# Splitting the shared rotary keys of a head pair as one bank, fifth score matmul over 64 rows, and shorter rsqrt chains in a single-core MLA kernel

## The chip, the cores and the metric

The kernel runs on one core of a Trainium2 chip. The metric is device time in microseconds of one execution. The core has a matrix engine (PE, with its weight loads listed apart as PEld), a vector engine (DVE), an activation engine (ACT), a general engine (POOL, also called GpSimd) and a sync engine (SP) whose queue issues nearly all DMAs. Each engine works through its own instructions in order; semaphores tie the engines together.

## The reference

Two layers over 512 tokens of width 2048: a pooling mixer, then multi-head latent attention with 16 heads. Only the attention matters here. Each head has 128 plain and 64 rotary channels; the rotary key is one for all heads, and the norm of a head's key runs over all 192 channels, so each head scales the same rotary key by its own factor.

```python
def shared_kv(x, kv_norm_g, kv_w_a, kv_latent_g, kv_w_b, k_norm_g, cos, sin):
    ...
    k_rope = jnp.broadcast_to(k_rope[:, :, None, :], (B, S, N_HEADS, QK_ROPE))
    k = qk_norm_rope(jnp.concatenate([k_nope, k_rope], axis=-1), k_norm_g, cos, sin)
    return k, v

def qk_norm_rope(t, g, cos, sin):
    t = rmsnorm(t, g)        # t * rsqrt(mean(t * t) + 1e-6) * g, over 192 channels
    return jnp.concatenate([t[..., :QK_NOPE], apply_rope(t[..., QK_NOPE:], cos, sin)], axis=-1)

def chunk_causal_attention(q, k, v):
    for i in range(S // QBLOCK):                 # QBLOCK 128
        s = jnp.einsum('bqhd,bkhd->bhqk', q[:, q0:k_end], k[:, :k_end]) * QK_HEAD ** -0.5
        ...
        p = jax.nn.softmax(s, axis=-1)
        outs.append(jnp.einsum('bhqk,bkhd->bqhd', p, v[:, :k_end]))
```

## The kernel before

All products are of float32 data that are split into a high and a low part (`hi` by a cast on ACT, `lo` = source - `hi` by a subtraction on DVE); a product is the sum of three matmuls, hi x hi, hi x lo and lo x hi. `split` (L154) does this for a whole tile.

The attention stage works on pairs of heads, `hg` = 0 to 7. The main loop (from about L1074) goes through 64 score units: pair, head `h` of the pair, block `i` of 128 queries. For each it emits the scores (`score_unit`), the exponential (`exp_unit`, ACT), the scaling by the reciprocal of the sum (`scale_unit`, DVE), the transposes of the scaled tile (`pt_unit`) and, for every second unit, the product with the values (`pv_unit`). Between these parts stand pieces of projections for the next pair (`kv_part`, `q_part`; in the last pair, pieces of the output projection), so that PE has work while the softmax runs. Preparations of the next pair are put at fixed units by the table `side`: `kstats_unit` behind unit 2, `krot_unit` behind unit 3, `tr_unit` 2 (the rotary keys) behind unit 5, `qstats_unit` and `tr_unit` 3 behind unit 6, `tr_unit` 5 (the rotary queries) in unit 7. The order of PE is that of the code, pinned by hand (`PINNED`). The order on ACT, DVE, POOL and SP is set by the tile scheduler, which places each instruction by its own model of when its inputs are there.

What the change touches:

- `kstats_unit` and `qstats_unit`, once a pair each: the factor 1/sqrt of 8 means per partition (4 token blocks x 2 heads), with `rsqrt` (L161): a first value by a shift of the float's bits, and three Newton steps of three instructions each (L166 to L168), on tiles of 128x8. With the scalings around it this makes 16 DVE instructions for k (four of them at L705, one for each token block) and 13 for q.
- `krot_unit` (L720, POOL) multiplies the shared rotary key by the factors of both heads, side by side in one tile.
- `tr_unit` with u = 2: four transposes (L754) put the rotary keys of both heads into one PSUM bank, head 0 in rows 0 to 63, head 1 in rows 64 to 127. Then, per head, two ACT casts of 64x512 (L763 and L764) write the high part twice, into rows 0 to 63 and 64 to 127 of a tile `kh`; DVE (L765) writes the low part into rows 0 to 63 of `kl`, and POOL (L762) zeros rows 64 to 127 of `kl`.
- `tr_unit` with u = 5: the rotary queries; per head one tile with the high part in rows 0 to 63 (L781) and the low part in rows 64 to 127 (L782).
- `score_unit` (L810): five matmuls into one bank. The first three are those of the plain channels. The fourth multiplies the tile of q (high over low) by `kh` (high over high), which gives two of the three rotary products at once; the fifth multiplies the same tile by `kl` (low over zeros).

`tr()` hands out two PSUM banks in turn to all transposes (of keys, queries and scaled tiles alike): a transpose waits until the bank's reader two uses before is through. `bt()` hands out 32 buffers of 128x512 in turn.

Numbers of lines are those of the kernel before; where a line of the changed kernel is meant, the text says so.

Of the kernel before, what the change touches and what calls it, by code (L numbers as in the profile page):

```python
# [7 lines left out]
F32 = mybir.dt.float32  # L8
F32R = mybir.dt.float32r
I32 = mybir.dt.int32  # L10
AF = mybir.ActivationFunctionType
ALU = mybir.AluOpType
AX = mybir.AxisListType

P = 128
S = 512
# [6 lines left out]
EPS = 1e-6  # L23
# [24 lines left out]
def trunk_kernel(  # L48
# [17 lines left out]
    V, A, G, T = nc.vector, nc.scalar, nc.gpsimd, nc.tensor  # L66

    const = ctx.enter_context(tc.tile_pool(name="const", bufs=1))
    rpool = ctx.enter_context(tc.tile_pool(name="rpool", bufs=2))
# [3 lines left out]
    def xt(shape=(P, S), dt=F32):  # L73
        return xpool.tile(list(shape), dt, tag="x", name="xt")
# [4 lines left out]
    def at(dt=F32R, shape=(P, S)):  # L79
        return apool.tile(list(shape), dt, tag="a", name="at")  # L80

    def bt(shape=(P, S), dt=F32R):
        return bpool.tile(list(shape), dt, tag="b", name="bt")
# [16 lines left out]
    def f(ap):  # L100
        return ap.bitcast(F32)
# [51 lines left out]
    def split(src, hi, lo):  # L153
        return A.copy(hi, src), V.tensor_tensor(lo, src, f(hi), ALU.subtract)  # L154
# [6 lines left out]
    def rsqrt(v, y, a, n):  # L161

        V.tensor_scalar(y.bitcast(I32), v.bitcast(I32), -0.5, float(0x5F3759DF), ALU.mult, ALU.add)
        V.tensor_scalar(v, v, -0.5, None, ALU.mult)
        for _ in range(3):
            V.tensor_tensor(a, y, y, ALU.mult)  # L166
            V.tensor_tensor(a, a, v, ALU.mult)
            V.scalar_tensor_tensor(y, a, 1.5, y, ALU.add, ALU.mult)  # L168
# [98 lines left out]
    with ExitStack() as c1:  # L267
# [106 lines left out]
        with ExitStack() as c2:  # L374
            hp = c2.enter_context(tc.tile_pool(name="hp", bufs=2, **tile_))
            for j in range(NJ):
# [5 lines left out]
                hi = w7.tile([P, 4, 2, P], F32R, tag="hi", name="hi")  # L382
                lo = w7.tile([P, 4, 2, P], F32R, tag="lo", name="lo")
# [10 lines left out]
                a, b = xh[j], xl[j]  # L394
# [11 lines left out]
        for o in range(0, 4, 2):  # L406
            e = epool.tile([P, 7, H], F32, tag="e", name="e")
            for i in range(2):
                v = e[:, 2 * i:2 * i + 2, :]
# [16 lines left out]
        for n, pair in enumerate((*range(18, 32), *range(16))):  # L426
# [7 lines left out]
            if n == 9:  # L434
                V.tensor_tensor(sq[0], sq[0], sq[1], ALU.add)
                p = ps7[0].tile([P, 2, H], F32, tag="k3", name="k3").rearrange("p h t -> p (h t)")
# [79 lines left out]
    for k in range(KD):  # L516
        hi, lo = at(), at()
        gsplit(xr[k], C_GKV + k, hi, lo)
        xkv.append((hi, lo))
        hi, lo = bt(), bt()  # L520
# [67 lines left out]
    kr = krb[:, 0:256].rearrange("p (t d) -> p t d", t=4)  # L588
# [6 lines left out]
    kr2 = const.tile([P, 4], F32, name="kr2")  # L595
# [34 lines left out]

    gqk = const.tile([P, 1], F32, name="gqk")
    V.tensor_tensor(gqk, cs[:, C_GKN:C_GKN + 1], cs[:, C_GQN:C_GQN + 1], ALU.mult)
    SC = 192.0 ** -0.5
    st, gated = {}, {}
    nhg = NH // 2

# [57 lines left out]
    def q_squares(hg, t):  # L694
        d = st[hg]
        for h in range(2):
            junk = spool.tile([P, 192], mybir.dt.bfloat16, tag="junk", name="junk", bufs=2)
            A.activation(junk, d["qraw"][t][:, h, :], AF.Square, accum_out=d["ssq"][:, 2 * t + h:2 * t + h + 1])

    def kstats_unit(hg):  # L700

        d = st[hg]
        v, a, y = small(8, "sv", 2), small(8, "sa", 2), small(8, "sy", 2)
        for t in range(4):
            V.tensor_scalar(v[:, 2 * t:2 * t + 2], d["ssk"][:, 2 * t:2 * t + 2], kr2[:, t:t + 1], None, ALU.add)  # L705
        V.tensor_scalar(v, v, 1.0 / 192, EPS, ALU.mult, ALU.add)
        rsqrt(v, y, a, 8)
        d["yk"] = y
        for a in range(2):
            kk = d["kraw"][a].rearrange("p b (h c) -> p (b h) c", h=2)  # L710
            V.tensor_tensor(kk, kk, y[:, 4 * a:4 * a + 4].unsqueeze(2).broadcast_to([P, 4, P]), ALU.mult)
# [11 lines left out]
    def qstats_unit(hg):  # L723

        d = st[hg]
        v, a, y = small(8, "qv", 2), small(8, "qa", 2), small(8, "qy", 2)
        V.tensor_scalar(v, d["ssq"], 1.0 / 192, EPS, ALU.mult, ALU.add)
        rsqrt(v, y, a, 8)
        V.tensor_scalar(y, y, SC, None, ALU.mult)
        d["rq"] = y  # L730

    def qrot_unit(hg, t):
# [13 lines left out]
    def tr_unit(hg, u):  # L746

        d = st[hg]
        if u == 2:

            d["kr"] = []
            p = tr()
            for t in range(4):
                T.transpose(p[:, t * P:(t + 1) * P], d["krs"][:, t * P:(t + 1) * P], ident)  # L754
            for h in range(2):
                src = p[h * 64:h * 64 + 64, :]
                if hg:
                    kh = bt()
                else:
                    kh = xt(dt=F32R) if h else rpool.tile([P, S], F32R, tag="r", name="kr0")  # L760
                kl = bt()
                G.memset(f(kl[64:128, :]), 0.0)  # L762
                A.copy(kh[0:64, :], src)  # L763
                A.copy(kh[64:128, :], src)  # L764
                V.tensor_tensor(kl[0:64, :], src, f(kh[0:64, :]), ALU.subtract)  # L765
                d["kr"].append((kh, kl))
            return
        p = tr()
        for t in range(4):
            if u < 2:  # L770
                src = d["kraw"][t // 2][:, t % 2, u * P:(u + 1) * P]
            elif u < 5:
                src = d["qraw"][t][:, u - 3, 0:128]
            else:
                src = d["qrot"][:, t * P:(t + 1) * P]
            T.transpose(p[:, t * P:(t + 1) * P], src, ident)  # L776
        if u == 5:
            q0, q1 = bt(), bt()
            for h, q in enumerate((q0, q1)):
                src = p[h * 64:h * 64 + 64, :]  # L780
                A.copy(q[0:64, :], src)  # L781
                V.tensor_tensor(q[64:128, :], src, f(q[0:64, :]), ALU.subtract)  # L782
            d["qr"] = (q0, q1)
            return
        ft = at if hg == 0 and u in (0, 3) else bt
        hi, lo = ft(), ft()
        if u in (3, 4):
            A.activation(hi, p, AF.Copy, scale=gqk)
            V.scalar_tensor_tensor(lo, p, gqk, f(hi), ALU.mult, ALU.subtract)
        else:  # L790
            split(p, hi, lo)
        d[("T", u)] = (hi, lo)

    def score_unit(hg, h, i):
        d = st[hg]
        n = (i + 1) * P
        if i == 2:

            gt = d[("G", h)] = bt(dt=F32)
            nc.sync.dma_start(gt, gates[2 * hg + h])  # L800
        s = sc()
        kh, kl = d[("T", h)]
        krh, krl = d["kr"][h]
        qh, ql_ = d[("T", 3 + h)]
        qr = d["qr"][h]
        qs = slice(i * P, (i + 1) * P)
        ops = [(qh[:, qs], kh[:, 0:n]), (qh[:, qs], kl[:, 0:n]), (ql_[:, qs], kh[:, 0:n]),
               (qr[:, qs], krh[:, 0:n]), (qr[:, qs], krl[:, 0:n])]
        for j, (l, r) in enumerate(ops):
            T.matmul(s[:, 0:n], l, r, start=(j == 0), stop=(j == 4))  # L810
        V.memset(s[0:64, n - 64:n], -1e30)
        nm = small(1, "nm", 4)
        V.tensor_reduce(nm, s[:, 0:n], AX.X, ALU.max)
        rq = d["rq"][:, 2 * i + h:2 * i + h + 1]
        V.scalar_tensor_tensor(nm, nm, -1.0, rq, ALU.mult, ALU.mult)
        d[("P", h, i)] = s, nm, rq
# [207 lines left out]
    for m, (key, w) in enumerate(keys):  # L1024
        n = last[keys[m - 4][0]] if m >= 4 else -1
# [48 lines left out]
    for m in range(len(seq) + 2):  # L1074
        now = seq[m] if m < len(seq) else None
        if now:
            hg, h, i = now
# [105 lines left out]
```

## Time and profile before

| what | us |
|---|---|
| runs | 1920.48, 1920.28, 1922.47 (median 1920.48) |
| the profiled execution | 1920.45 |
| its span, from first to last instruction | 1918.7 |
| attention stage, pairs 1 to 7 | about 1480 to 1765 of the span |
| one steady pair | 35.2 |

The profile is of one execution. Instructions are listed with the line that made them, the tile written and the tiles read, partitions x columns, a start and a duration. PE's instructions are pipelined: a matmul's listed duration overlaps the next, so the distance between two starts is what counts, and a distance longer than usual is a stall. Here are three stretches of the score loop, in windows (length; busy time and number of PE, PEld, DVE, ACT and POOL; clock; DMA share; GB/s):

```profile
1541.70:1577.00 35.30, 35.16 (x218) 31.69 (x218) 31.05 (x108) 27.43 (x91) 9.71 (x20) 1.00 0.25 79
1647.40:1682.60 35.20, 35.05 (x217) 31.67 (x216) 30.98 (x106) 27.35 (x90) 9.71 (x20) 1.00 0.27 83
1730.00:1765.00 35.00, 34.62 (x196) 29.98 (x195) 26.77 (x76) 19.23 (x49) 0.00 (x0) 1.00 0.43 124
```

The steady pairs are alike to a tenth of a microsecond. The last row is the last pair's second half, when no further pair is prepared; its POOL is empty.

### The profile page before, as it was taken

To read this page: it belongs to the slowest core of one execution; us is meant where nothing else is said; L and a number is where in the kernel's file an instruction comes from. 1 tells how busy PE (TensorE), PEld (TensorE's weight loads), DVE (VectorE), ACT (ScalarE), POOL (GpSimd) and SP (SyncE) were. 2 spreads that over 40 slices of the span, in tenths; PEclk is the share of its full clock that TensorE was granted. 3 is DMA by queue.
4 is the path that set the end of the run, shared out by engine and by line. 5 is a ranking of instruction groups with operands and counts; after the bars stand their busy time and mean duration, and the time that the engine had idled before them with its cause. 6 is when DMAs were issued, how large, how long until landed. Compare 5 with 4: busy or idle time off the path is not lost.

```text
span 1918.7 us, 30196 instructions
## 1 busy us (share of the span) xinstructions
PE 1902.5 (99%) x11084; PEld 1688.6 (88%) x11084; DVE 1299.6 (68%) x2282; ACT 829.2 (43%) x1555; POOL 286.9 (15%) x436
## 2 busy tenths in 40 slices
PE   8999999999999999999999999999999999999999
PEld 7999999999999988888888888888888888988887
DVE  8677796897766786586695576574335888887332
ACT  8444433333333442332432354233236787775221
POOL 0433343333232100000000000000001332320000
PEclk9999999999999999999999999999999999999999
DMA  6555444444454556334334344334443232244642
GB/s 191 158 162 159 150 132 133 123 129 138 145 151 131 167 172 199 115 119 152 118 124 137 105 150 132 93 99 121 116 120 95 82 96 77 74 128 143 200 117 87
DMA packets 177077, 251.24 MB, mean 131 GB/s; under 512 B 15776, under 2 KB 96800, under 8 KB 176928
## 3 DMA queue, kind: packets, MB, share of 16 engines
q1 hardware_dynamic: 176640, 249.10, 42.3%
q8 instruction: 87, 1.43, 0.3%
q14 instruction: 62, 0.51, 0.1%
q10 hardware_dynamic: 288, 0.20, 0.0%
HBM read 216.21 MB, written 33.03 MB: 130 GB/s over the span
## 4 chain that ended last, share of the span: by engine, by line
PE 93%; DVE 3%; DMA 2%; ACT 1%; issue 1%; POOL 0%; SPq 0%; DVEq 0%; POOLq 0%; ACTq 0%
PE mm L149 16%; PE mm L151 16%; PE mm L150 16%; PE k L346 10%; PE k L344 9%; PE k L342 9%; PE k L339 3%; PE sc L810 2%; PE mm L662 1%; PE mm L664 1%; PE mm L663 1%; PE mm L685 1%; PE mm L686 1%; PE mm L687 1%; PE tr L838 1%; PE tr L776 1%
## 5 line engine op out<-in xcount | busy, mean ns | idle before, releaser
L131 ACT CAST whi<-raw 128x512 fp32r<-128x512 f32 (+2 forms) x424 | 256.2, 607 | 539.4 <-PE mm L150 439.9
L132 DVE TENSOR_TENSOR wlo<-raw,whi 128x512 fp32r<-128x512 f32 (+2 forms) x424 | 283.8, 670 | 242.7 <-ACT whi L131 239.7
L346 PE MATMUL k<-xc,lo 128*128 128x256 f32 x1680 | 417.4, 283 | 0.8 <-DVE lo L320 0.8
L344 PE MATMUL k<-xc,hi 128*128 128x256 f32 x1440 | 397.5, 283 | 0.0
L342 PE MATMUL k<-xc,hi 128*128 128x256 f32 x1440 | 396.8, 282 | 0.0
L151 PE MATMUL mm<-bt,wlo 128*128 128x512 f32 x944 | 368.0, 390 | 0.0
L149 PE MATMUL mm<-bt,whi 128*128 128x512 f32 x944 | 367.7, 390 | 0.0
L150 PE MATMUL mm<-bt,whi 128*128 128x512 f32 x944 | 367.0, 389 | 0.0
L320 DVE TENSOR_TENSOR lo<-raw,hi 128x1792 fp32r<-128x1792 f32 x120 | 249.3, 2078 | 131.7 <-ACT hi L319 131.5
L319 ACT CAST hi<-raw 128x1792 fp32r<-128x1792 f32 x120 | 203.2, 1693 | 285.7 <-PE k L346 172.5
L346 PEld LDWEIGHTS k<-xc,lo 128*128 128x128 f32 x1680 | 302.7, 190 | 8.3 <-DVE lo L320 2.0
L342 PEld LDWEIGHTS k<-xc,hi 128*128 128x128 f32 x1440 | 273.3, 190 | 5.0
L344 PEld LDWEIGHTS k<-xc,hi 128*128 128x128 f32 x1440 | 273.7, 190 | 0.0
L151 PEld LDWEIGHTS mm<-bt,wlo 128*128 128x128 f32 x944 | 177.1, 188 | 37.3 <-issue 0.5
L149 PEld LDWEIGHTS mm<-bt,whi 128*128 128x128 f32 x944 | 177.3, 188 | 36.9 <-ACT whi L131 0.2
L150 PEld LDWEIGHTS mm<-bt,whi 128*128 128x128 f32 x944 | 177.2, 188 | 36.7
L150 PE MATMUL mm<-at,whi 128*128 128x512 f32 x432 | 168.6, 390 | 0.3 <-DVE at L154 0.3
L149 PE MATMUL mm<-at,whi 128*128 128x512 f32 x432 | 168.8, 391 | 0.0
L151 PE MATMUL mm<-at,wlo 128*128 128x512 f32 x432 | 168.2, 389 | 0.0
L315 POOL TENSOR_TENSOR raw<-raw 128x256 f32<-128x256 f32 x120 | 97.5, 812 | 428.3 <-DVE raw L313 410.1
L316 POOL TENSOR_TENSOR raw<-raw 128x256 f32<-128x256 f32 x120 | 110.0, 917 | 9.2
L150 PEld LDWEIGHTS mm<-at,whi 128*128 128x128 f32 x432 | 81.1, 188 | 17.3 <-DVE at L154 0.6
(1137 smaller groups left out, 2714.2 us busy)
## 6 DMA issues: line engine op xcount, KB each, us to landing
raw<-awin SPq DMA_DIRECT2D x240, 256.0 KB, 3.4
raw<-awo SPq DMA_DIRECT2D x128, 256.0 KB, 2.7
raw<-bwin SPq DMA_DIRECT2D x80, 256.0 KB, 2.9
raw<-awg SPq DMA_DIRECT2D x64, 256.0 KB, 2.7
scr<-e SPq DMA_DIRECT2D x56, 256.0 KB, 2.7
raw<-bwo SPq DMA_DIRECT2D x56, 256.0 KB, 2.9
raw<-wkvb SPq DMA_DIRECT2D x32, 256.0 KB, 3.1
raw<-wqb SPq DMA_DIRECT2D x32, 192.0 KB, 2.4
```

Source lines behind the costliest of these rows:

```text
L131: wsplits[:] = (A.copy(hi[:, :n], raw[:, :n]).ins, V.tensor_tensor(lo[:, :n], raw[:, :n], f(hi[:, :n]), ALU.subtract).ins)
L132: V.tensor_tensor(lo[:, :n], raw[:, :n], f(hi[:, :n]), ALU.subtract).ins)
L149: T.matmul(dst, wh, xh, start=first, stop=False)
L150: T.matmul(dst, wh, xl, start=False, stop=False)
L151: T.matmul(dst, wl, xh, start=False, stop=last)
L315: G.tensor_tensor(c[:, :, 6, :], c[:, :, 4, :], c[:, :, 2, :], ALU.add)
L316: G.tensor_tensor(c[:, :, 7, :], c[:, :, 6, :], c[:, :, 3, :], ALU.add)
L319: A.copy(hi, c[:, :, 1:8, :])
L320: V.tensor_tensor(lo, c[:, :, 1:8, :], f(hi), ALU.subtract)
L342: T.matmul(dst, hi[:, j % 2, wi, :], xh[j][:, xi, :], start=first, stop=False, skip_group_check=True)
L344: T.matmul(dst, hi[:, j % 2, wi, :], xl[j][:, xi, :], start=False, stop=False, skip_group_check=True)
L346: T.matmul(dst, lo[:, j % 2, wi, :], xh[j][:, xi, :], start=False, stop=last, skip_group_check=True)
```

## The change

It has three parts. **The split of the rotary keys** (`tr_unit`, u = 2): one cast and one subtraction take the whole bank of 128x512, with head 0 in the upper rows and head 1 in the lower. Three POOL copies of 64x512 then build what the fourth matmul needs: `k1` gets head 1's high part in both halves, and the lower half of `k0` is overwritten with head 0's; that last copy comes after DVE has read `k0`. `kl` holds the low parts of both heads; nothing is zeroed. A pair takes three `bt` buffers here, not four. **The fifth score matmul** reads 64 rows only: rows 0 to 63 for head 0, 64 to 127 for head 1. For that the queries of head 1 have their high part in rows 64 to 127 and the low part above it. **The rsqrt chains**: the factors -0.5, 1/192 and the eps are folded into one instruction per chain (with a constant tile `kr2b`, made once), and in place of three Newton steps come one step of a higher order, in four instructions, and one Newton step, in three. With the folding and the first value that makes 9 instructions for k and 9 for q.

```diff
@@ -630,7 +630,6 @@
 
     gqk = const.tile([P, 1], F32, name="gqk")
     V.tensor_tensor(gqk, cs[:, C_GKN:C_GKN + 1], cs[:, C_GQN:C_GQN + 1], ALU.mult)
-    SC = 192.0 ** -0.5
     st, gated = {}, {}
     nhg = NH // 2
 
@@ -697,14 +696,30 @@
             junk = spool.tile([P, 192], mybir.dt.bfloat16, tag="junk", name="junk", bufs=2)
             A.activation(junk, d["qraw"][t][:, h, :], AF.Square, accum_out=d["ssq"][:, 2 * t + h:2 * t + h + 1])
 
+    C3 = 3.375 ** 2
+    kr2b = const.tile([P, 4, 2], F32, name="kr2b")
+    V.tensor_scalar(kr2b, kr2.unsqueeze(2).broadcast_to([P, 4, 2]), -0.5 / (192 * C3), -0.5 * EPS / C3,
+                    ALU.mult, ALU.add)
+
+    def rsqrt_small(v, y, a):
+
+        V.tensor_scalar(y.bitcast(I32), v.bitcast(I32), -0.5, float(0x5F3759DF - 2 ** 30 - 2 ** 22),
+                        ALU.mult, ALU.add)
+        V.tensor_tensor(a, y, y, ALU.mult)
+        V.tensor_tensor(a, a, v, ALU.mult)
+        V.scalar_tensor_tensor(a, a, 5.0 / 3.0, a, ALU.add, ALU.mult)
+        V.scalar_tensor_tensor(y, a, 1.25, y, ALU.add, ALU.mult)
+        V.tensor_tensor(a, y, y, ALU.mult)
+        V.tensor_tensor(a, a, v, ALU.mult)
+        V.scalar_tensor_tensor(y, a, 2.0 / 3.0, y, ALU.add, ALU.mult)
+
     def kstats_unit(hg):
 
         d = st[hg]
         v, a, y = small(8, "sv", 2), small(8, "sa", 2), small(8, "sy", 2)
-        for t in range(4):
-            V.tensor_scalar(v[:, 2 * t:2 * t + 2], d["ssk"][:, 2 * t:2 * t + 2], kr2[:, t:t + 1], None, ALU.add)
-        V.tensor_scalar(v, v, 1.0 / 192, EPS, ALU.mult, ALU.add)
-        rsqrt(v, y, a, 8)
+        V.scalar_tensor_tensor(v, d["ssk"], -0.5 / (192 * C3), kr2b.rearrange("p t h -> p (t h)"),
+                               ALU.mult, ALU.add)
+        rsqrt_small(v, y, a)
         d["yk"] = y
         for a in range(2):
             kk = d["kraw"][a].rearrange("p b (h c) -> p (b h) c", h=2)
@@ -724,9 +739,8 @@
 
         d = st[hg]
         v, a, y = small(8, "qv", 2), small(8, "qa", 2), small(8, "qy", 2)
-        V.tensor_scalar(v, d["ssq"], 1.0 / 192, EPS, ALU.mult, ALU.add)
-        rsqrt(v, y, a, 8)
-        V.tensor_scalar(y, y, SC, None, ALU.mult)
+        V.tensor_scalar(v, d["ssq"], -0.5 / C3, -0.5 * 192 * EPS / C3, ALU.mult, ALU.add)
+        rsqrt_small(v, y, a)
         d["rq"] = y
 
     def qrot_unit(hg, t):
@@ -748,22 +762,19 @@
         d = st[hg]
         if u == 2:
 
-            d["kr"] = []
             p = tr()
             for t in range(4):
                 T.transpose(p[:, t * P:(t + 1) * P], d["krs"][:, t * P:(t + 1) * P], ident)
-            for h in range(2):
-                src = p[h * 64:h * 64 + 64, :]
-                if hg:
-                    kh = bt()
-                else:
-                    kh = xt(dt=F32R) if h else rpool.tile([P, S], F32R, tag="r", name="kr0")
-                kl = bt()
-                G.memset(f(kl[64:128, :]), 0.0)
-                A.copy(kh[0:64, :], src)
-                A.copy(kh[64:128, :], src)
-                V.tensor_tensor(kl[0:64, :], src, f(kh[0:64, :]), ALU.subtract)
-                d["kr"].append((kh, kl))
+            if hg:
+                k0, k1 = bt(), bt()
+            else:
+                k0, k1 = rpool.tile([P, S], F32R, tag="r", name="kr0"), xt(dt=F32R)
+            kl = bt()
+            split(p, k0, kl)
+            for half in (slice(0, 64), slice(64, 128)):
+                G.tensor_copy(k1[half, :], k0[64:128, :])
+            G.tensor_copy(k0[64:128, :], k0[0:64, :])
+            d["kr"] = (k0, kl[0:64, :]), (k1, kl[64:128, :])
             return
         p = tr()
         for t in range(4):
@@ -778,9 +789,10 @@
             q0, q1 = bt(), bt()
             for h, q in enumerate((q0, q1)):
                 src = p[h * 64:h * 64 + 64, :]
-                A.copy(q[0:64, :], src)
-                V.tensor_tensor(q[64:128, :], src, f(q[0:64, :]), ALU.subtract)
-            d["qr"] = (q0, q1)
+                hi, lo = q[h * 64:h * 64 + 64, :], q[64 - h * 64:128 - h * 64, :]
+                A.copy(hi, src)
+                V.tensor_tensor(lo, src, f(hi), ALU.subtract)
+            d["qr"] = (q0, q0[0:64, :]), (q1, q1[64:128, :])
             return
         ft = at if hg == 0 and u in (0, 3) else bt
         hi, lo = ft(), ft()
@@ -802,10 +814,10 @@
         kh, kl = d[("T", h)]
         krh, krl = d["kr"][h]
         qh, ql_ = d[("T", 3 + h)]
-        qr = d["qr"][h]
+        qr, qrh = d["qr"][h]
         qs = slice(i * P, (i + 1) * P)
         ops = [(qh[:, qs], kh[:, 0:n]), (qh[:, qs], kl[:, 0:n]), (ql_[:, qs], kh[:, 0:n]),
-               (qr[:, qs], krh[:, 0:n]), (qr[:, qs], krl[:, 0:n])]
+               (qr[:, qs], krh[:, 0:n]), (qrh[:, qs], krl[:, 0:n])]
         for j, (l, r) in enumerate(ops):
             T.matmul(s[:, 0:n], l, r, start=(j == 0), stop=(j == 4))
         V.memset(s[0:64, n - 64:n], -1e30)
```

PE's instructions stand in the same sequence as before. The order of the other engines moves. First ACT at a boundary between two steady pairs, where the rotary keys of the next pair are split: `bt<-tr 64x512` are the casts of the keys, `sc` the scores, `xt<-tr` the tiles of the transposed softmax. Before:

```order
L850 CAST xt<-tr 128x128
L763 CAST bt<-tr 64x512
L764 CAST bt<-tr 64x512
L823 ACTIVATE tt__15937,sm<-sc,nm,qy 128x256
L763 CAST bt<-tr 64x512
L764 CAST bt<-tr 64x512
L154 CAST at<-mm 128x256
L823 ACTIVATE tt__15993,sm<-sc,nm,qy 128x384
```

The same place in the changed kernel:

```order
L862 CAST xt<-tr 128x128
L154 CAST bt<-tr 128x512
L835 ACTIVATE tt__15887,sm<-sc,nm,qy 128x256
L154 CAST at<-mm 128x256
L835 ACTIVATE tt__15939,sm<-sc,nm,qy 128x384
```

One cast stands ahead of the exp of 256 columns where two stood, and none between it and the next exp. In the pair at 1505 us the one cast stands behind the exp of 256 columns, where the first of the four stood.

Second DVE at the same place. `qv`, `qy` and `qa` are the tiles of the q chain, `nm` the maximum of a score tile, `sm` the sum of an exp. Before:

```order
L727 TENSOR_SCALAR qv<-ssq 128x8
L852 TENSOR_TENSOR xt<-tr,xt 128x128
L163 TENSOR_SCALAR qy<-qv 128x8
L164 TENSOR_SCALAR qv<-qv 128x8
L166 TENSOR_TENSOR qa<-qy 128x8
L765 TENSOR_TENSOR bt<-tr,bt 64x512
L167 TENSOR_TENSOR qa<-qa,qv 128x8
L811 MEMSET sc 64x64
L829 RECIPROCAL sm<-sm 128x1
L168 SCALAR_TENSOR_TENSOR qy<-qa,qy 128x8
L813 TENSOR_REDUCE nm<-sc 128x1
L830 TENSOR_SCALAR tt__15937<-tt__15937,sm 128x256
```

In the changed kernel:

```order
L742 TENSOR_SCALAR qv<-ssq 128x8
L864 TENSOR_TENSOR xt<-tr,xt 128x128
L706 TENSOR_SCALAR qy<-qv 128x8
L154 TENSOR_TENSOR bt<-tr,bt 128x512
L708 TENSOR_TENSOR qa<-qy 128x8
L841 RECIPROCAL sm<-sm 128x1
L823 MEMSET sc 64x64
L709 TENSOR_TENSOR qa<-qa,qv 128x8
L842 TENSOR_SCALAR tt__15887<-tt__15887,sm 128x256
L825 TENSOR_REDUCE nm<-sc 128x1
L710 SCALAR_TENSOR_TENSOR qa<-qa 128x8
```

The scaling of the exp tile (L830, now L842) has moved ahead of the search for the next maximum (L813, now L825). In the pair at 1505 us it stands ahead of the subtraction of the keys in both kernels.

Third DVE in the last pair, around 1722 us, from the subtraction for an output weight on (`wlo`). Before:

```order
L132 TENSOR_TENSOR wlo<-raw,whi 128x256
L166 TENSOR_TENSOR qa<-qy 128x8
L811 MEMSET sc 64x64
L765 TENSOR_TENSOR bt<-tr,bt 64x512
L813 TENSOR_REDUCE nm<-sc 128x1
L167 TENSOR_TENSOR qa<-qa,qv 128x8
L815 SCALAR_TENSOR_TENSOR nm<-nm,qy 128x1
L168 SCALAR_TENSOR_TENSOR qy<-qa,qy 128x8
L166 TENSOR_TENSOR qa<-qy 128x8
L167 TENSOR_TENSOR qa<-qa,qv 128x8
L765 TENSOR_TENSOR bt<-tr,bt 64x512
```

In the changed kernel:

```order
L132 TENSOR_TENSOR wlo<-raw,whi 128x256
L154 TENSOR_TENSOR bt<-tr,bt 128x512
L712 TENSOR_TENSOR qa<-qy 128x8
L823 MEMSET sc 64x64
L713 TENSOR_TENSOR qa<-qa,qv 128x8
L825 TENSOR_REDUCE nm<-sc 128x1
L714 SCALAR_TENSOR_TENSOR qy<-qa,qy 128x8
```

The reading of the keys' bank ends with the one subtraction, at the place of the first L765; the second, seven rows later, is gone.

On POOL the memsets, which waited for nothing but a free buffer, are gone; the three copies stand behind the pair's last rotary query (L744, now L758) and wait for ACT's cast, the third for DVE's subtraction too. `krot_unit`'s two products come ahead of the last instruction of a rotary query, not behind it. On SP two things change, both late: a load of a gate comes ahead of a load of the output weights, and a store of a gated tile behind a load of another.

## The prediction

> **What bounds the kernel now.** I read the engines' busy line first, then the table by windows, then every gap between starts on PE from 1480 us on (where the pairs of heads follow each other), and last the timeline around those gaps.
>
> ```profile
> span 1918.7 us, 30196 instructions
> PE 1902.5 (99%) x11084; PEld 1688.6 (88%) x11084; DVE 1299.6 (68%) x2282; ACT 829.2 (43%) x1555; POOL 286.9 (15%) x436
> ```
>
> PE is busy for 99% of the span, so work that is taken from DVE or ACT is worth nothing by itself. Only a place where PE stands still for one of them can pay. The windows of the attention stage (columns: length, then the busy time and count of PE, PEld, DVE, ACT and POOL, the clock, DMA share, GB/s) say how much there is:
>
> ```profile
> 1577.00:1612.20 35.20, 35.06 (x218) 31.66 (x216) 30.98 (x107) 27.36 (x91) 9.70 (x20) 1.00 0.29 87
> 1682.60:1730.00 47.40, 44.77 (x266) 39.26 (x265) 41.94 (x144) 36.67 (x112) 9.44 (x20) 1.00 0.40 126
> ```
>
> A steady pair lasts 35.20 us, of which PE is busy for 35.06; the granted clock is 1.00, so no time can come back from there. The stretch into the last pair has 2.63 us without PE. Each of its stalls has to be looked at alone. The largest two have the same cause, the split of the rotary keys (ACT L763 and L764, DVE L765, each once per head):
>
> ```profile
> 1506.50 0.57 ACT L763 CAST bt<-tr 64x512 fp32r<-64x512 f32 x1
> ...
> 1509.01 0.39 PE L664 MATMUL mm<-wlo,at 128*128 128x512 f32 x1
> 1509.67 0.69 DVE L765 TENSOR_TENSOR bt<-tr,bt 64x512 fp32r<-64x512 f32 x1
> 1510.51 0.63 PE L776 MATMUL tr<-cs,qt 128*128 128x128 f32 x4 [1.11 <-DVE qy L168]
> ...
> 1721.88 0.68 DVE L765 TENSOR_TENSOR bt<-tr,bt 64x512 fp32r<-64x512 f32 x1
> ...
> 1722.71 0.38 PE L838 MATMUL tr<-cs,tt__18213 128*128 128x128 f32 x2
> 1723.81 0.69 DVE L765 TENSOR_TENSOR bt<-tr,bt 64x512 fp32r<-64x512 f32 x1
> 1724.65 0.63 PE L776 MATMUL tr<-cs,qt 128*128 128x128 f32 x4 [1.56 <-DVE qy L168]
> ```
>
> L776 transposes into one of the two `tr` banks, and the bank it gets is the one that the second L765 still reads. That L765 ends at 1510.36 and 1724.50, and PE goes on 0.15 us behind it. (The name behind the arrow, L168, is the small instruction that happened to end nearest; it writes nothing that L776 reads.) Two matmuls of 512 columns start 0.23 us apart when nothing holds them, so the first stall is 1.50 - 0.23 = 1.27 us. Two transposes of 128 columns take 0.17 us of PE (L838 at 1580.03, the next matmul at 1580.20, in the fence below), so the second is 1.94 - 0.17 = 1.77 us. **Together 3.04 us.**
>
> In the five pairs between, the same split costs less and by another way:
>
> ```profile
> 1576.95 0.58 ACT L763 CAST bt<-tr 64x512 fp32r<-64x512 f32 x1 [0.81 <-PE tr L754]
> 1577.54 0.58 ACT L764 CAST bt<-tr 64x512 fp32r<-64x512 f32 x1
> 1578.14 0.56 ACT L823 ACTIVATE tt__15937<-sc,nm,qy 128x256 f32<-128x256 f32 x1
> 1578.15 0.68 DVE L765 TENSOR_TENSOR bt<-tr,bt 64x512 fp32r<-64x512 f32 x1 [0.55 <-ACT bt L764]
> 1579.49 0.40 PE L664 MATMUL mm<-wlo,at 128*128 128x512 f32 x1
> 1579.54 0.34 DVE L830 TENSOR_SCALAR tt__15937<-tt__15937,sm 128x256 f32<-128x256 f32 x1
> 1580.03 0.41 PE L838 MATMUL tr<-cs,tt__15937 128*128 128x128 f32 x2
> ...
> 1580.20 0.48 PE L662 MATMUL mm<-whi,at 128*128 128x512 f32 x1
> ```
>
> The exp of the tile stands on ACT behind two casts, its scaling (L830) on DVE behind L765, and the transposes of that tile (L838) start at 1580.03 instead of 1579.49 + 0.23 = 1579.72: 0.31 us. The other four pairs read alike (L664 to L838 is 0.53 or 0.54 us), so **1.5 us in all**. What the kernel can gain from the split is at most 3.04 + 1.54 = 4.6 us.
>
> **The change part by part.** *The split.* Per pair, four casts of 64x512 become one of 128x512, and two subtractions of 64x512 become one of 128x512.
>
> ```profile
> L763 ACT CAST bt<-tr 64x512 fp32r<-64x512 f32 x14 | 8.1, 580 | 5.8 <-PE tr L754 4.0 <-DVE bt L765 1.5
> L765 DVE TENSOR_TENSOR bt<-tr,bt 64x512 fp32r<-64x512 f32 x14 | 9.6, 688 | 3.1 <-ACT bt L764 2.8
> L154 ACT CAST bt<-tr 128x512 fp32r<-128x512 f32 x15 | 9.1, 607 | 0.0
> L154 DVE TENSOR_TENSOR bt<-tr,bt 128x512 fp32r<-128x512 f32 x15 | 10.2, 682 | 0.0
> ```
>
> Twice the rows cost nothing: ACT goes from 4 x 0.58 = 2.32 to 0.61 us, DVE from 1.38 to 0.68 us. The bank is then free after one cast and one subtraction. In the pair at 1509 the changed order has the cast where the first L763 stood, from 1506.50, and the subtraction behind it ends by about 1508.2 with some small instructions between, a good microsecond before PE wants the bank at 1509.24. In the last pair the subtraction comes where the first L765 stood (1721.88), ending near 1722.6, and PE comes at 1722.88: 0.3 us of cover, thin but enough. I take both stalls as gone, **-3.04 us**.
>
> *The copies on GpSimd.* The second head's tile and the lower copy of the first are now made by three copies of 64x512, SBUF to SBUF; two memsets go. The trace has no such copy. The rows nearest:
>
> ```profile
> L762 POOL MEMSET bt<- 64x512 f32 x14 | 7.3, 521 | 0.8
> L720 POOL TENSOR_TENSOR tt__18067<-krr,sy 128x256 f32<-128x256 f32 x2 | 1.2, 616 | 0.0
> ```
>
> A memset of the same shape writes as much and reads nothing, 0.52 us: the lower end. A product of two inputs takes 0.616 us for 256 columns where DVE leaves it alone, twice that, 1.23 us, for 512: the upper end, since a copy reads one input. I take 0.60, near the memset, which has the same shape. POOL has time (9.70 of 35.20 us busy), and the keys are first read by the next pair's scores, which come after the rest of this pair's: some microseconds of cover. The price lies elsewhere: POOL and DVE hold each other up.
>
> ```profile
> 1505.31 0.46 POOL L744 TENSOR_TENSOR tt__14568<-tt__14568,tt__14569 128x128 f32<-128x128 f32 x1
> 1505.37 0.43 DVE L727 TENSOR_SCALAR qv<-ssq 128x8 f32<-128x8 f32 x1
> ...
> 1576.90 0.15 DVE L727 TENSOR_SCALAR qv<-ssq 128x8 f32<-128x8 f32 x1
> ```
>
> L727 takes 0.15 us alone (beside a memset of POOL, even), 0.43 us when it meets a POOL product, and it ends when that ends. I count L765 and other readers of PSUM as not held (0.68 or 0.69 us in every row above), nor the reciprocal. The Trainium skill has this as a rule, in "SBUF — State Buffer", section "SBUF: two separate sides": a DVE operation in a two-port mode, or with two SBUF inputs against a GpSimd one that reads SBUF, waits for the whole of the other, and the other for it. The rows above agree for the products; no run here shows it for a copy, and if a copy didn't hold the lock, the sum would be rival A's.
>
> The changed order puts the scaling of the steady pair right into the copies: on DVE come subtraction, L708, reciprocal, memset, L709, scaling (new line numbers). With the first cast from 1576.95 to 1577.56 the copies start near 1577.70. Take c for one copy. L708 waits for copy 1, copy 2 for L708 (0.1 us), L709 for copy 2, copy 3 for L709 (0.1), the scaling (0.34) for copy 3: it ends at 1577.70 + 3c + 0.54, and PE's L838 starts some 0.13 us on, at 1578.37 + 3c. That is today's 1580.03 at c = 0.55, and the stall is gone (1579.72) at c = 0.45. The change per pair is 3 x (c - 0.553), never below -0.31. At 0.60 it is +0.14, times five pairs **+0.7 us**; at 0.52 -0.5, at 1.0 +6.7, at 1.23 +10.2. The casts' gain is taken back by the copies, and the 0.31 us stays or grows.
>
> *The rsqrt chains.* 16 small DVE instructions become 9 for k, 13 become 9 for q.
>
> ```profile
> L705 DVE TENSOR_SCALAR sv<-ssk,kr 128x2 f32<-128x2 f32 x28 | 6.3, 224 | 1.7 <-ACT junk L674 1.7
> L166 DVE TENSOR_TENSOR qa<-qy 128x8 f32<-128x8 f32 x21 | 3.3, 159 | 0.0
> L150 PEld LDWEIGHTS mm<-at,whi 128*128 128x128 f32 x112 | 21.1, 188 | 4.7 <-DVE at L154 0.6
> ```
>
> That is some 3 x 0.22 + 4 x 0.16 = 1.3 us and 4 x 0.16 = 0.64 us a pair. PE covers it: the scores that use these values come microseconds later. A little may come back where PE waits for a DVE that is behind (0.6 us at L150 in the last row); I take **-0.2 us**, between 0 and -0.6.
>
> *The fifth score matmul over 64 rows.* 64 matmuls now have 64 rows of weights; columns and count stay, so I see no gain. PE must change its shape before and behind each, 128 changes. The latent stage of before already alternates shapes, 128x64 and 128x128 weights, and beside it stands the plain run:
>
> ```profile
> 1230.03 0.39 PE L578 MATMUL mm<-at,whi 128*64 128x512 f32 x1
> 1230.26 0.40 PE L579 MATMUL mm<-at,whi 128*128 128x512 f32 x1
> ...
> 1235.32 0.39 PE L150 MATMUL mm<-bt,whi 128*128 128x512 f32 x1
> 1235.55 0.39 PE L151 MATMUL mm<-bt,wlo 128*128 128x512 f32 x1
> ...
> 1574.54 0.28 PE L869 MATMUL ov<-xt,at 128*128 128x128 f32 x1
> 1574.65 0.27 PE L870 MATMUL ov<-xt,at 128*128 128x128 f32 x1
> ```
>
> Starts are 0.23 us apart in both, so a change of columns costs nothing. Rows are not shown. The lower end is 0; the upper is a pipe that must run empty: 0.27 us of a matmul less the 0.11 us between two starts, 0.16 us, x 128 = 20 us. I take 0, by the one change of shape that the trace has.
>
> **Sum:** -3.04 + 0.7 - 0.2 = -2.5 us against the profiled execution (1920.45 us, span 1918.7), within 0.03 us of the median 1920.48. **1918.0 us.** A measurement of this kernel tells about 0.2%, 3.8 us, from no change: faster means below 1916.6, slower above 1924.3.
>
> **The rivals.** *A: all stalls of the split go.* If a copy takes 0.45 us or less, or doesn't hold DVE up, the five stalls go too: -3.04 - 1.54 - 0.2 = -4.8, 1915.7 us; with the rest of DVE's stalls 1915.3. For it: only 0.15 us of c. Against: the memset, which only writes, has 0.52. *B: long copies.* Above c = 0.77 the five pairs lose more than the 3.24 us; at 1.0 it is +3.5 (1923.9), at 1.23 +7.0 (1927.4). For it: the products of POOL; slower by the measure from about c = 1.03. *C: the changes of rows empty PE.* At half the upper price, 0.08 us, 128 changes cost 10 us: 1928 us; it decides from 0.05 us a change (6.3 us). Against it stands the row pair above. The Trainium skill, in "TensorEngine Tiling (Array Packing)", section "Key Properties", says that changing the tiling mode drains TensorE. It names column modes too, and L578 and L579 show no drain, so the trace speaks against it there; for rows no run shows it. *D: no gain.* A PE that comes earlier to the last pairs waits for weights:
>
> ```profile
> 1703.99 0.41 PE L838 MATMUL tr<-cs,tt__17902 128*128 128x128 f32 x2 [0.66 <-DVE sc L811]
> ...
> SPq L933 <- PE mm L664: 12.3, 1, 12.3
> ```
>
> Ahead of this start lies a wait for weights, whose load stands in SP's queue behind one (L933) that has waited 12.3 us for PE; so part of it moves with PE's own pace. If the 3.04 us are given back to loads here and behind, the time is 1920.45 + 0.7 - 0.2 = 1921.0 us.
>
> **How the numbers follow.** Chances: the forecast with c of 0.45 to 0.8, 0.62; A 0.14; B 0.09; C 0.08; D 0.07. The range 1915.4 to 1923.9 takes in the forecast, A but its end, D, and B up to c = 1.0; longer copies, C and a little of A are left out, 0.2. Faster: A and an eighth of the forecast, 0.22. Slower: C, and B but a little, 0.16. Same: 0.62.
>
> **What would show it.** Right: the gaps before the transposes of q's head at 1509 and 1722 are gone, the copies take near 0.6 us, and in each steady pair DVE's small instructions and the scaling end with a copy, with PE's L838 still 0.3 to 0.5 us late. Wrong: steady gaps gone or above 1 us (c mis-sized); more than 0.25 us between the starts around the fifth score matmul, in all 64 places (C); a new wait of PE for a load (D).

## The result, and the profile after

The changed kernel takes 1939.13 us (median of 4 runs, 1938.57 to 1939.35), the kernel before 1921.26 us beside it: ratio 1.009, 95% interval 1.0075 to 1.0105. It is slower by 18 us, where 1918.0 us and a range up to 1923.9 were forecast.

The profiled execution took 1939.35 us. Its page, the same lines as of before, shows PE with 21 us more of busy time for the same 11084 matmuls, and DVE and ACT relieved as meant:

```profile
span 1937.6 us, 30070 instructions
PE 1923.5 (99%) x11084; PEld 1691.1 (87%) x11084; DVE 1281.7 (66%) x2187; ACT 818.8 (42%) x1531; POOL 285.5 (15%) x444
```

The time isn't in stalls of PE, which are fewer than before, but in the steady pairs themselves. Two of them, cut at the first small instruction behind the keys' subtraction (columns as in the windows of before):

```profile
1548.51:1586.25 37.74, 37.74 (x217) 31.97 (x216) 28.78 (x94) 25.91 (x87) 9.42 (x22) 1.00 0.24 76
1586.25:1624.03 37.78, 37.78 (x217) 32.01 (x216) 28.73 (x94) 26.01 (x87) 9.43 (x22) 1.00 0.26 80
```

A pair took 35.20 us before and takes 37.78 now, at full clock, with PE never idle. What has grown are the score matmuls. The groups by shape, for 384 columns (count, busy us and mean ns of one), and beside them the start of one score unit, matmuls and weight loads together:

```profile
L822 PE MATMUL sc<-bt 128*128 128x384 f32 x59 | 12.8, 337 | 0.0
...
L822 PE MATMUL sc<-bt 64*128 64x384 f32 x16 | 7.0, 439 | 0.0
```

```profile
1604.51 0.71 PEld L822 LDWEIGHTS sc<-bt 128*128 128x128 f32 x4
1604.68 1.23 PE L822 MATMUL sc<-bt 128*128 128x384 f32 x5
1605.47 0.18 PEld L822 LDWEIGHTS sc<-bt 64*128 64x128 f32 x1 [0.25 <-issue]
1605.84 0.19 PEld L684 LDWEIGHTS mm<-whi,at 128*128 128x128 f32 x1 [0.19 <-issue]
1605.84 0.44 PE L684 MATMUL mm<-whi,at 128*128 128x384 f32 x1
1605.95 0.19 PEld L685 LDWEIGHTS mm<-whi,at 128*128 128x128 f32 x1
1606.12 0.34 PE L685 MATMUL mm<-whi,at 128*128 128x384 f32 x1
```

The same unit in the kernel before:

```profile
1595.37 0.88 PEld L810 LDWEIGHTS sc<-bt 128*128 128x128 f32 x5
1595.54 1.03 PE L810 MATMUL sc<-bt 128*128 128x384 f32 x5
1596.23 0.19 PEld L685 LDWEIGHTS mm<-whi,at 128*128 128x128 f32 x1
1596.41 0.33 PE L685 MATMUL mm<-whi,at 128*128 128x384 f32 x1
1596.58 0.33 PE L686 MATMUL mm<-whi,at 128*128 128x384 f32 x1
```

Before, each weight load begins one matmul (0.17 us) ahead of the matmul that needs it, and the next projection starts 0.87 us after the first score matmul. In the changed kernel the weight load of the 64 rows begins only when its matmul does, at 1605.47; the fourth matmul began at 1605.20, and 384 columns take 0.174 us, so for 0.09 us PE starts nothing. The matmul's record is 0.10 us longer (0.44 for 0.34), and the next matmul comes that much later; I read it as the load. Behind it the same again: the load of L684 begins together with its matmul at 1605.84, another 0.10 us, after another 0.09 us in which PE starts nothing. Whether the array is empty in these gaps the trace doesn't tell: ends of matmuls are modelled, and the record of the fourth runs on to 1605.54. The distance grows from 0.87 to 1.16 us, and the one from L684 to L685 from 0.17 to 0.28 us. That is 0.39 us for this unit. Units of 256 and 512 columns pay the same, units of 128 columns 0.29 us (medians of 16 units each, from the starts in both traces).

### The profile page after: what moved, and what is told of

Its sections match the earlier page's. It is cut to its first block, busy times and chain, and to the rows that moved or that the text cites. A ratio compares the mean times of both kernels' runs of the same rounds, so it can differ in the third digit from the quotient of the medians.

```text
span 1937.6 us, 30070 instructions
## 1 busy us (share of the span) xinstructions
PE 1923.5 (99%) x11084; PEld 1691.1 (87%) x11084; DVE 1281.7 (66%) x2187; ACT 818.8 (42%) x1531; POOL 285.5 (15%) x444
## 4 chain that ended last, share of the span: by engine, by line
PE 95%; DVE 2%; DMA 1%; ACT 1%; issue 1%; SPq 0%; POOL 0%; DVEq 0%; ACTq 0%; POOLq 0%
PE mm L150 16%; PE mm L149 16%; PE mm L151 16%; PE k L346 10%; PE k L344 9%; PE k L342 8%; PE sc L822 3%; PE k L339 3%; PE mm L661 2%; PE mm L663 2%; PE mm L662 2%; PE mm L684 1%; PE mm L685 1%; PE mm L686 1%; PE tr L787 1%; PE tr L850 1%
```

## Experiments

The theory from the trace (S): a change of PE between weights of 128 and of 64 rows costs about 0.19 us, half of it a gap in which PE starts nothing, half a weight load with nothing beside it. The rivals put part of the 18 us on the copies and the new order (P), on the copies' hold of DVE (L), or on each matmul of 64 rows (M).

**The whole change, but the fifth matmul over 128 rows** (the first run, below). The order on all engines is that of the changed kernel.

```diff
-            d["kr"] = (k0, kl[0:64, :]), (k1, kl[64:128, :])
+            d["kr"] = (k0, kl), (k1, kl)
...
-            d["qr"] = (q0, q0[0:64, :]), (q1, q1[64:128, :])
+            d["qr"] = (q0, q0), (q1, q1)
```

> The changed kernel with its fifth score matmul over all 128 rows again: it multiplies the whole tile of the rotary queries by the whole tile of the low parts, so one head's low query part meets the other head's low key part, a product that is added here and lies near the last bits. Nothing else differs, and the order on every engine is that of the changed kernel. Theory S (each change of PE between 128 and 64 rows of weights costs about 0.09 us in which PE runs empty and about 0.1 us of a weight load that can't be done beside the matmul before, some 0.19 us x 128 = 24 us): all of that goes, the spacing of the fourth and fifth matmul of a 384-column score returns from 0.268 to 0.174 us, the time falls to 1914.5 to 1917. Rival P (part of the 18 us is paid by the copies on GpSimd or the new order): the time stays above 1922. Rival L (the steady pairs' stall of 0.31 us returns as soon as PE is fast enough, since the copies hold DVE up, as forecast): about 1918, with L850 0.3 to 0.5 us late in the five steady pairs.

Measured: 1918.09 us (11 runs), ratio 0.9987 (0.9978 to 0.9995). So 21 us come back with the rows alone, and nothing of the 18 us is left for the copies or the new order: P falls. But it is 1 us above what S expected. Of the five stalls of rival L there is no trace: in the steady pair the transposes come at their time (L663 at 1579.64, L850 at 1579.88). A new wait stands elsewhere, ahead of the transposes of the 512-column tile. PE and ACT there:

```profile
1532.91 0.37 ACT L697 ACTIVATE junk<-qt 128x192 bf16<-128x192 f32 x1
1533.16 0.21 ACT L697 ACTIVATION_READ_ACCUMULATOR junk<-qt 128x1 f32 x1
1533.26 0.79 ACT L835 ACTIVATE tt__15175<-sc,nm,qy 128x512 f32<-128x512 f32 x1
...
1534.89 0.34 PE L686 MATMUL mm<-wlo,at 128*128 128x384 f32 x1
1535.33 0.41 PE L850 MATMUL tr<-cs,tt__15175 128*128 128x128 f32 x2
```

L850 should start 0.17 us after L686 and starts 0.44 us after it: 0.27 us, in five pairs alike, and 1.16 us in the first.

**The kernel before, only with 64 rows in the fifth matmul.**

```diff
-               (qr[:, qs], krh[:, 0:n]), (qr[:, qs], krl[:, 0:n])]
+               (qr[:, qs], krh[:, 0:n]), (qr[0:64, qs], krl[0:64, 0:n])]
```

> The kernel before with one edit: the fifth score matmul reads rows 0 to 63 of the two tiles (the other rows are zeros, so the product is the same). Theory S: 128 changes at 0.19 us are 24 us, of which the stalls of before (7.0 us in all, waits for ACT, DVE and loads) hide 2 to 5 us because PE comes later to them: 1939.5 to 1943. Rival P: within 4 us of the kernel before.

Measured: 1938.85 us, ratio 1.0094 (1.008 to 1.0108): 18 us from one slice in one line. It is 0.7 us under the expected range. The trace has the rows at the same 0.36 us a unit, 23.2 us in all where 24 were taken, and PE's stalls behind 1480 us fell from 6.9 to 1.9 us, the most that was allowed for. Both heads read rows 0 to 63 here, so the price doesn't hang on which half of the rows is read.

**The fifth matmul twice.** The low product counts double here.

```diff
-               (qr[:, qs], krh[:, 0:n]), (qrh[:, qs], krl[:, 0:n])]
+               (qr[:, qs], krh[:, 0:n]), (qrh[:, qs], krl[:, 0:n]), (qrh[:, qs], krl[:, 0:n])]
...
-            T.matmul(s[:, 0:n], l, r, start=(j == 0), stop=(j == 4))
+            T.matmul(s[:, 0:n], l, r, start=(j == 0), stop=(j == 5))
```

> The changed kernel with the fifth score matmul issued twice in succession, both over the same 64 rows; the low product is added twice. Theory S (the price is for the change of rows, not for a matmul of 64 rows): the second costs its columns alone, 0.06, 0.12, 0.17 and 0.23 us for the four sizes, 0.145 us x 64 = 9.3 us, to 1948 to 1950, and its weight load begins beside the first. Rival M (each matmul over 64 rows has a price of its own, because its weights are never loaded ahead): 0.145 + 0.2 to 0.37 us x 64 = 22 to 33 us, 1961 to 1972.

Measured: 1947.12 us, ratio 1.0136 (1.0122 to 1.015), 8.0 us above the changed kernel and 0.9 us under the range of S. The scheduler's order on ACT and DVE is not the same here, and waits of PE that the changed kernel has are shorter by 1.4 us (0.86 us at the first pair is gone, 1.0 us near 1750 is 0.42 us). With these the difference is 9.4 us, near the 9.3 us of the columns: a second matmul of 64 rows costs its columns and no more, and M falls. Its weight load is done ahead again (two loads in 0.29 us from 1607.70, next full load only at 1608.24):

```profile
1607.09 1.23 PE L822 MATMUL sc<-bt 128*128 128x384 f32 x5
1607.26 0.19 PEld L822 LDWEIGHTS sc<-bt 128*128 128x128 f32 x1
1607.70 0.29 PEld L822 LDWEIGHTS sc<-bt 64*128 64x128 f32 x2 [0.25 <-issue]
1608.24 0.19 PEld L684 LDWEIGHTS mm<-whi,at 128*128 128x128 f32 x1 [0.25 <-issue]
```

**The short rsqrt chains alone, in the kernel before.** The edit is the part of the change in `kstats_unit` and `qstats_unit`.

> The kernel before with the short rsqrt chains alone (9 DVE instructions in place of 16 and 13); split of the keys and score matmuls as before. Theory: the two large stalls ahead of the query transposes (1.27 and 1.77 us) and the five of 0.31 us stay, since they hang on the casts and subtractions of the keys; 1919 to 1920.5. Rival: the shorter chains alone let DVE come in time, the second L765 ends early enough, and 2 us or more go: 1918.5 or less.

Measured: 1923.1 us (11 runs), ratio 1.0009 (1.0000 to 1.0018). Both expectations miss. Of the old stalls, the one of 1.7 us and the five of 0.3 us stay, as the theory had it, but the one of 1.27 us is 0.44 us here; and the new waits of 1.15 and five times 0.27 us are here too. So these belong to the chains, not to the split. DVE in the first run shows what has moved. `L726` are the two scalings of the keys by the k chain's result:

```profile
1530.02 0.15 DVE L714 SCALAR_TENSOR_TENSOR sy<-sa,sy 128x8 f32<-128x8 f32 x1
1530.20 1.29 DVE L726 TENSOR_TENSOR at<-at,sy 128x512 f32<-128x512 f32 x2
1531.50 0.11 DVE L823 MEMSET sc<- 64x64 f32 x1
1531.64 0.69 DVE L825 TENSOR_REDUCE nm<-sc 128x1 f32<-128x512 f32 x1
1532.37 0.42 DVE L827 SCALAR_TENSOR_TENSOR nm<-nm,qy 128x1 f32<-128x1 f32 x1
```

and in the kernel before:

```profile
1530.64 0.11 DVE L811 MEMSET sc<- 64x64 f32 x1 [0.18 <-PE sc L810]
1530.67 0.15 DVE L167 TENSOR_TENSOR sa<-sa,sv 128x8 f32<-128x8 f32 x1
1530.79 0.69 DVE L813 TENSOR_REDUCE nm<-sc 128x1 f32<-128x512 f32 x1
1531.40 0.16 DVE L168 SCALAR_TENSOR_TENSOR sy<-sa,sy 128x8 f32<-128x8 f32 x1
1531.52 0.16 DVE L815 SCALAR_TENSOR_TENSOR nm<-nm,qy 128x1 f32<-128x1 f32 x1
1531.59 1.71 DVE L711 TENSOR_TENSOR at<-at,sy 128x512 f32<-128x512 f32 x2
```

The shorter chain is through before the scores are ready, so the scheduler puts 1.29 us of scalings into the gap, ahead of the maximum. The maximum then ends at 1532.79 instead of 1531.68, and on ACT the exp of 512 columns is placed behind two casts and two squares: 1533.26 instead of 1532.20. This is theory K, and four runs test it.

**Split without chains; q chain alone; k chain alone.** All three with the fifth matmul over 128 rows. The first has the long chains of before in the first run's kernel, the second puts back only the long k chain, the third only the long q chain.

> The kernel before with the new split of the keys and the three copies, but the long rsqrt chains and the fifth score matmul over all 128 rows (over the whole tile of low parts, as in the first run). Theory K (the short k chain, not the split, brings the new waits: with it DVE does the two scalings of the keys, 1.29 us, ahead of the search for the maximum of 512 columns, and the exp of 512 columns falls behind two casts and two squares on ACT, so that PE waits 1.16 us in the first pair and 0.27 us in each of five): none of these here, and the stalls of the old split (1.27, 1.77, five of 0.31 us) gone too: 4 to 5 us faster than before, 1915.5 to 1917. Rival: the order of the split itself brings them: 1918 as in the first run, with the five waits of 0.27 us.

> The first run's kernel (whole change, fifth score matmul over 128 rows) with the long chain of before for k alone; the q chain is short. Theory K: as without short chains, no wait of 0.27 us, 1915 to 1916.5, at least 2 us under the first run's 1918.1. Rival Q (it is the q chain): 1918 with the waits of 0.27 us.

> The mirror image: the first run's kernel with the long chain of before for q alone; the k chain is short. Theory K: the waits of 1.16 us and of 0.27 us in five pairs are there, 1917.5 to 1919. Rival Q: they are gone, 1915 to 1916.5.

Measured: 1915.98 us without short chains (ratio 0.9971, 0.9960 to 0.9982), 1915.84 us with the short q chain (0.9970, 0.9959 to 0.9982), 1917.81 us with the short k chain (0.9986, 0.9977 to 0.9995). In the first two the waits of 0.27 us are absent, in the third all are there. The short q chain is worth nothing that can be measured, and the short k chain costs about 2 us. Those 2 us are less than two times of this kernel can be told apart by; what carries them is the trace, where the waits make 2.5 us. The split alone, without the change of rows, gains 5 us, more than the 0.2% that can be told.

One wait came with the new split and was not forecast. It is ahead of the transposes of a 512-column tile in the last pair, here in the changed kernel:

```profile
1749.96 0.63 PE L850 MATMUL tr<-cs,tt__18261 128*128 128x128 f32 x4 [0.94 <-DVE tt__18261 L842]
```

The same place costs 0.3 us in the kernel before, 1.0 us in the changed kernel, and 1.25 to 1.46 us in the first run and the three runs above. In all of these but the kernel before, the exp of that tile stands on ACT behind the two casts of the transposed tile ahead of it; in the kernel before it stands ahead of them, and so it does in the run with the fifth matmul twice, with 0.42 us. No run changes this order alone, so the cause is argued, not shown.

**Both chains short, the scalings behind the maximum.** The scalings leave `kstats_unit`, are emitted behind the scores of unit 3, and are ordered behind the maximum:

```diff
+    def kscale_unit(hg):
...
+            ins = V.tensor_tensor(kk, kk, y[:, 4 * a:4 * a + 4].unsqueeze(2).broadcast_to([P, 4, P]), ALU.mult)
+            if "nm" in st:
+                tc.add_manual_dep(ins.ins, st["nm"].ins.name, ...)
...
-... (2, 1): [(0, tr_unit, 4), (1, kstats_unit)], (3, 1) ...
+... (2, 1): [(0, tr_unit, 4), (1, kstats_unit)], (3, 0): [(1, kscale_unit)], (3, 1) ...
```

> The first run's kernel (whole change, both chains short, fifth score matmul over 128 rows) with one edit in the order of DVE: the two scalings of the keys stand behind the maximum of the 512 columns again, not ahead of it. Theory K by order (the short k chain harms only because its scalings come ahead of the maximum and the exp falls behind the squares on ACT): the wait of 1.16 us and the five of 0.27 us go, 1915 to 1916.5, with as many DVE instructions as in the first run. Rival (the short chain itself, or the time at which it ends, makes PE wait): 1917.5 to 1919, the waits stay.

Measured: 1915.55 us (7 runs, 1914.65 to 1918.64), ratio 0.9973 (0.9962 to 0.9984). The waits of 1.16 and 0.27 us are gone with the short chain in place, so it was the order. (The traced execution took 1918.01 us: from 63.4 to 66.8 us of its span, far ahead of the attention stage, the granted clock was 0.50.) The exp of 512 columns stands ahead of the casts again (L842 at 1533.10, the casts of L869 at 1533.87), and a steady pair is as short as its PE work:

```profile
1543.86:1578.74 34.88, 34.88 (x218) 31.77 (x217) 28.93 (x95) 25.78 (x87) 10.04 (x22) 1.00 0.27 84
```

This version, the split without chains and the one with the short q chain can't be told apart; all three are faster than both kernels.

**The copies as products with ones.** Same values, and the order of PE, ACT, DVE and SP is that of the first run. It tests why rival L's stall didn't come.

```diff
+        G.tensor_tensor(v(dst), f(v(src)), one.unsqueeze(1).broadcast_to([64, 4, P]), ALU.mult)
...
-                G.tensor_copy(k1[half, :], k0[64:128, :])
-            G.tensor_copy(k0[64:128, :], k0[0:64, :])
+                gcopy(k1[half, :], k0[64:128, :], ones[64:128, :])
+            gcopy(k0[64:128, :], k0[0:64, :], ones[0:64, :])
```

> The first run's kernel with the three copies on GpSimd made as products with a tile of ones: same values, same order on every engine, but two inputs read from SBUF instead of one. Theory H (a GpSimd instruction with two inputs holds DVE up, a copy doesn't, which is why the forecast wait of 0.3 to 0.5 us in the steady pairs did not come): the products take 1.2 us or more each, DVE's small instruction L709 and the scaling L842 behind the keys' subtraction grow from 0.16 and 0.34 us to 0.4 or more, and PE's transposes of that tile come 0.5 to 2 us late in each steady pair: 1921 to 1929. Rival (nothing holds DVE up there): DVE's durations as in the first run and the time within 1.5 us of it.

Measured: 1926.68 us (10 runs), ratio 1.0027 (1.0018 to 1.0036), 8.6 us above the first run. DVE and PE in the steady pair, with products (first fence) and with copies (second):

```profile
1580.42 0.82 DVE L708 TENSOR_TENSOR qa<-qy 128x8 f32<-128x8 f32 x1
...
1581.38 1.37 DVE L846 TENSOR_SCALAR tt__15887<-tt__15887,sm 128x256 f32<-128x256 f32 x1
...
1581.72 0.40 PE L663 MATMUL mm<-wlo,at 128*128 128x512 f32 x1
1582.89 0.41 PE L854 MATMUL tr<-cs,tt__15887 128*128 128x128 f32 x2 [0.77 <-DVE tt__15887 L846]
```

```profile
1577.83 1.26 POOL L775 CAST bt<-bt 64x512 fp32r<-64x512 f32 x2 [1.72 <-ACT bt L154]
1578.34 0.16 DVE L708 TENSOR_TENSOR qa<-qy 128x8 f32<-128x8 f32 x1
1578.76 0.35 DVE L709 TENSOR_TENSOR qa<-qa,qv 128x8 f32<-128x8 f32 x1
1579.03 0.34 DVE L842 TENSOR_SCALAR tt__15887<-tt__15887,sm 128x256 f32<-128x256 f32 x1
1579.15 0.69 POOL L776 CAST bt<-bt 64x512 fp32r<-64x512 f32 x1
...
1579.64 0.40 PE L663 MATMUL mm<-wlo,at 128*128 128x512 f32 x1
1579.88 0.38 PE L850 MATMUL tr<-cs,tt__15887 128*128 128x128 f32 x2
```

The three products take 1.27 to 1.32 us each and PE comes 0.9 to 1.0 us late in each steady pair, as H said (of the small instructions it is L708 that grows, not L709). But H was wrong in saying that a copy doesn't hold DVE: in the first run L709 takes 0.35 us and ends, at 1579.11, 0.02 us behind the second copy. A copy holds too; it is short enough not to matter here. Five pairs make 4.7 of the 8.6 us. Of the rest 0.4 us lie in the first pair, and 1.1 us in the stall in the last pair named above, which is 2.36 us here, ending at 1738.57, and 1.25 in the first run. Behind that stall the clock falls (windows; the clock is the third number from the end):

```profile
1736.00:1739.30 3.30, 1.10 (x10) 0.95 (x10) 3.20 (x10) 2.75 (x7) 0.00 (x0) 1.00 0.85 266
1739.30:1743.00 3.70, 3.70 (x11) 2.89 (x10) 2.33 (x8) 1.13 (x4) 0.00 (x0) 0.54 0.30 95
```

PE idled for 2.2 of 3.3 us, and then for 3.7 us its granted clock was 0.54: another 1.7 us. All ten runs show a mean clock of 0.999, all of the first run 1.0. That leaves 0.7 us open.

## Why the prediction was wrong

**The step that failed** is the fifth score matmul, "I take 0, by the one change of shape that the trace has". That change was one of columns, 128 to 64, and it doesn't stand for a change of rows. The changed kernel's steady pair is 37.78 us against 34.88 with the rows put back and no wait left (the run with the scalings behind the maximum): 2.90 us for 8 score matmuls, 0.36 us each, 0.18 per change, 23 us over 64. Rival C had the change of rows as the cause, but half its size (0.08 us a change, 1928 us), and with 0.08 hardly any chance. The upper bound of 0.16 us a change was too low as well: it was all for an array that runs empty, where the gap measures 0.09 us, and it left out the weight load that is no longer done beside a matmul (0.10 us). The Trainium skill's "TensorEngine Tiling (Array Packing)", section "Key Properties", says that a change of the tiling mode drains TensorE. For rows the trace agrees in that each change costs time, though it doesn't show the drain itself; for columns L578 and L579 still speak against it.

**The two large stalls, -3.04 us**: right. They are absent in the changed kernel and in every run with the new split. (The second is 1.72 us rather than 1.77, since a transpose of 128 columns starts 0.11 us behind another.) The forecast didn't see that 0.7 us or more of this comes back as a longer wait a little later in the last pair.

**The copies, c = 0.60 us**: right in size; they take 0.61 to 0.69 us. The +0.7 us made from it was wrong. The forecast let the scaling wait for the third copy; in the trace it follows L709 on DVE at once, at 1579.03, and the third copy starts behind it. Of DVE's rows there only L709 is longer, by 0.2 us, beside the second copy, and the five stalls of 0.31 us are gone: rival A was right about the split. The rule cited from the Trainium skill, "SBUF — State Buffer", section "SBUF: two separate sides", agrees for a copy as well (L709, 0.35 us for 0.16).

**The rsqrt chains, -0.2 us**: wrong in sign. The instructions are shorter, as counted, but the order that they leave to the scheduler costs about 2 us in the run with the rows put back. The orders on ACT and DVE around the k chain were there to be read before the forecast; I looked at them only where the keys are split.

**The sum** of the profiled executions: PE's stalls behind 1480 us are 6.9 us before and 2.3 now (0.86 at the first pair, 0.42 at 1733 us, 1.0 at 1750 us). That is -4.6 us, and with 23.2 for the rows the attention stage should grow by 18.6 us. PE's matmuls come in the same sequence in both kernels; the changed kernel's are 1.4 us later than before at 1480 us and 19.3 us later at the end, so the stage has grown by 17.9 us, and 0.7 us stay open. Of the 1.4 us, 1.1 arise in the first 80 us of the span, which none of the edits touches. In the changed kernel the five waits of 0.27 us don't show, since PE comes late to them.

That the first run lands on 1918.1, the time forecast, is luck: about -5 us came from the split and +2 from the k chain, where the forecast had -3.04 from the split, +0.7 from the copies and -0.2 from the chains.

## What to carry to other kernels

Matmuls over fewer rows save nothing in PE time when the columns stay, and each change between row counts costs 0.18 us here: group them, or pad to 128 rows with whatever operand is harmless. When a kernel is bound by one engine, fewer instructions on another can change its time through the order that they lead to, here for the worse; read that order at every wait of the bound engine, not only where the diff is. Before a neighbouring row of the trace is taken for a price, ask whether it changes the same thing.

## What the runs showed of the hardware

- Changing PE from weights of 128 rows to 64 and back, at 256 columns and more: 0.09 us in which it starts nothing and 0.10 us of weight load that isn't done beside the matmul ahead, each time. Between two matmuls of the same 64 rows the load is done ahead (1607.81, its matmul 1607.98, in the run with the fifth matmul twice).
- A change between 128 and 64 columns of weights (L578 and L579, starts 0.23 us apart, each load begun 0.2 us ahead of its matmul) shows neither.
- After a stretch of 3.3 us with PE busy for 1.1 us, the granted clock was 0.54 for the next 3.7 us, in the run with products on GpSimd; in the run with the scalings behind the maximum, 1.4 us busy of 3.3 came ahead of 3.4 us at 0.50. The kernel before's stall of 1.77 us, 1.74 us busy of 3.3 around it, had no such echo.
- A GpSimd copy of 64x512 from SBUF to SBUF takes 0.61 to 0.69 us, a product of two inputs of that shape 1.27 to 1.35 us in the steady pairs. Both can make a DVE instruction that reads SBUF last until they end (0.35 us for 0.16 beside a copy; 0.82 for 0.16 and 1.37 for 0.34 beside a product). Not each one is held: L709, 0.35 us beside the copy, took 0.15 us beside the product.
